# Seven products for twelve more pairs of a feed-forward, sixteen modulation steps moved to another one, and a new order in three short places

## The chip, the cores and the metric

The kernel is one program on one core of a Trainium2 chip. The metric is device time of that core in microseconds (us), the median of several executions. TensorE (PE in the profile, with PEld for its weight loads) does the matrix products, VectorE (DVE), ScalarE (ACT) and GpSimd (POOL) the elementwise work, and SyncE (SP) issues most of the transfers from the chip's memory into the on-chip buffer. Each engine takes its instructions in the order in which the program has them and waits at one whose inputs are not there.

## The reference, cut to what matters

Two layers work on 512 tokens, 256 latent ones (`x`) and 256 of context (`xc`), of width 1024. Each layer is a feed-forward, a mixing block and another feed-forward. All is fp32.

```
mod = (silu(c) @ ada_w[l] + ada_b[l])                 # nine vectors of 1024 per layer, for x and for xc
h   = rms(x) * (1 + mod[1]) + mod[0]
x   = x + 0.5 * mod[2] * ((silu(h @ wg) * (h @ wu)) @ wd)       # wg, wu: 1024 x 2816, wd: 2816 x 1024
h   = rms(x) * (1 + mod[4]) + mod[3]
x   = x + mod[5] * mixing(h)    # short and long convolution, gated chunk MLP, latent attention
x   = x + 0.5 * mod[8] * (second feed-forward, with mod[6], mod[7])
```

The chunk MLP of the mixing multiplies a normalised `v` (in the kernel `gv`) by a 128 x 128 matrix per group (in the kernel in `sg`). In the second layer the mixing and the last feed-forward need the latent tokens alone.

## The kernel before, in words

Tokens lie along the free dimension, features on the 128 partitions. The program runs its stages one after the other: first feed-forward (layer 0; `ffn(0,0)`), mixing, second feed-forward (`ffn(0,1)`), then for layer 1 the third feed-forward (`ffn(1,0)`), the last mixing and a fourth feed-forward over 256 tokens.

Every fp32 product is made of three products in a rounded fp32 format, high by high, low by high and high by low (`mm3`, lines 164 to 166). So each weight block is loaded into `raw` by a transfer that SP issues, cast to `whi` by ACT, and DVE makes `wlo` as `raw` minus `whi` (`split`, line 139). `raw`, `whi` and `wlo` have four buffers each.

A feed-forward cuts its 2816 inner columns into 22 blocks of 128. Block m is a pair of products, gate and up, each over eight blocks of 128 features: 2 x 8 x 3 = 48 matrix products of 512 columns. The pairs go in three chunks, 0 to 7, 8 to 14 and 15 to 21. After each chunk comes its down projection: eight output tiles d, each a sum over the chunk's blocks in a `dn` bank (two of them), after which DVE adds the tile to `x` (`residual`, line 583).

In the pairs that the table `SEVEN` lists, the pair's product with its 2 x 2 blocks of halves is made with seven block products in place of eight (the Strassen-Winograd form): 7 x 12 = 84 matrix products of 256 columns. It needs sums of the weights (`raw`, `ws`, `w3h`, `w3l`: DVE and POOL) and sums of `h`, as `th` and `tl`, which `forms` makes by four subtractions for each of four tiles. Before, `SEVEN` has 15 pairs of the third feed-forward alone.

Beside this, each feed-forward does a share of the modulation: 128 steps (`ada_sums`) in all. One step loads 512 KB of `ada_w` into `araw` (SP) and does two instructions on DVE, `asum <- araw, cc, asum`, one for each half of a vector's columns, or one where the vector is needed for latent tokens only. After every eighth step PE gathers the partitions with `pick` (line 239), and two transposes and a few small DVE operations make the modulation vector `modv`. `slot(n)`, called once per pair and once per down tile, does n steps. The four feed-forwards do 48, 40, 32 and 8 steps. The first two also make the filters of a mixing (`filters`, in buffers named `filt`), a little in each slot.

Across engines nothing else orders the work: within each engine the framework's scheduler places instructions by priorities and the dependencies, so the order on an engine can differ from the order of the code. The changed places are `ada_sums`, `full` and `forms` of the class `Modulated`, `ffn`, and the section of `mixing` with `short` (six projections for the short convolution, line 971), two projections for `gu` and the products with `sg` (line 992).

Of the kernel before, what the change touches and what calls it, by code (L numbers as in the profile page):

```python
# [26 lines left out]
SEVEN = {(1, 0): tuple(range(4, 7)) + tuple(range(8, 14)) + tuple(range(15, 21))}  # L27
# [57 lines left out]
def tile_trunk(ctx: ExitStack, tc: tile.TileContext, xT, cT, ada_f, ada_w, w_up, w_dn, w_in, w_v, w_uq, w_ukv, w_out,  # L85
# [123 lines left out]
    here, rows, sums = [], [], []  # L209
# [12 lines left out]
    def ada_sums(n, tile_of):  # L222

        for _ in range(n):
            l, m, k, raw = here.pop(0)
            S = halves_of(l, m)
            with queued(later):
# [7 lines left out]
            if k == KD - 1:  # L235
                p = bank("ad", 1)
                for s in range(S):
                    for q in range(4):
                        PE.matmul(p[32 * q:32 * q + 32, 0:256], lhsT=pick[:, s, :],
                                  rhs=sums[s][:, q * 256:(q + 1) * 256], start=(s == 0), stop=(s == S - 1))  # L240
                sums.clear()
                row = tp.tile([P, 256], F32, tag="arow", name="arow", bufs=2)
                A.copy(out=row, in_=p[:, :256])
                rows.append((l, m, row))
# [48 lines left out]
    class Modulated:  # L293
# [51 lines left out]
        def full(self, b, bc, k, anchors):  # L345
# [5 lines left out]
            for i in range(2):  # L351
                if self.keep is None:
                    t = tp.tile([P, 512], F32, tag="t0", name="nt")
                else:
                    t = self.kept[-1][:, i * 512:(i + 1) * 512]
                eng, src = (V, b) if k + i == 0 else (G, bc)
                eng.tensor_tensor(out=t[:, :T], in0=x[:, ks[i], :T], in1=src[:, :T], op=ALU.mult)  # L357
                ts.append(t)
            for i, t in enumerate(ts):
                for s, c in enumerate(halves(T)):  # L360
                    g, h = (modv[self.l][:, self.m + j, s, ks[i]:ks[i] + 1] for j in (1, 0))
                    if i == 0:
                        A.activation(t[:, c], t[:, c], AF.Identity, bias=h, scale=g)
                    else:
                        V.tensor_scalar(out=t[:, c], in0=t[:, c], scalar1=g, scalar2=h, op0=ALU.mult, op1=ALU.add)
# [4 lines left out]
        def forms(self, th, tl):  # L370
# [215 lines left out]
    def ffn(l, f, T, h, nxt, steps, side=None):  # L586

        m0 = 6 * f
        with ExitStack() as es:
            fx = es.enter_context(tc.tile_pool(name=f"side{l}{f}", bufs=1, reuse_waits="tile"))  # L590
            fpool = es.enter_context(tc.tile_pool(name=f"ffn{l}{f}", bufs=1, reuse_waits="tile"))
            fast = SEVEN.get((l, f), ())
            af = [fpool.tile([P, 8 * 516], F32R, name=n) for n in ("ah", "al")]
# [8 lines left out]
            def tile_b():  # L602
                return fx.tile([P, 1024], F32, tag="filt", name="filt", bufs=7)

            def tile_w():
                return fpool.tile([P, 1024], F32, tag="ws", name="ws", bufs=1)

            if fast:
                th = fpool.tile([P, 4, 1028], F32R, name="th")
                tl = fpool.tile([P, 4, 1028], F32R, name="tl")  # L610
# [8 lines left out]
            else:  # L619
                hh, hl = h.high, h.low  # L620
                n = 3 if T == 512 else 4
                if fast:
# [6 lines left out]
            def slot(n):  # L629
                ada_flush()  # L630
                for _ in range(min(n, left[0])):
# [5 lines left out]
                if n > 0 or calm == 2:  # L637
                    next(gen, None)

            def todo_light():  # L640
                return not here or halves_of(*here[0][:2]) == 1
# [9 lines left out]
            def copied(src):  # L651
                t = fpool.tile([P, 256], F32, tag="cp", name="cp", bufs=5)
# [720 lines left out]
```

## Time and profile before

| | |
|---|---|
| median of 3 executions | 1780.89 us (1779.01 to 1781.73) |
| the profiled execution: own time, span | 1781.89 us, 1780.1 us |
| busy share of the span | PE 97%, PEld 82%, DVE 71%, ACT 41%, POOL 14% |
| stages on the profile's clock | first feed-forward 0 to 423 us, mixing to 658, second feed-forward to 1046.6, third to 1415.4, last mixing to 1570, fourth feed-forward to the end |
| transferred | 254.65 MB, mean 143 GB/s |

Busy is the time in which an engine has an instruction under way; a busy PE is not one at its peak, since its clock is granted in levels. The span is the time from the profile's first instruction to its last; the own time is that of the same execution as the device reports it.

### The profile page before, as it was taken

What the parts mean: (1) busy time and instruction counts of PE and PEld (TensorE: products, weight loads), DVE (VectorE), ACT (ScalarE), POOL (GpSimd) and SP (SyncE); (2) the same over time, 40 slices, a digit from 0 to 9 for tenths busy, and PEclk for the clock granted to TensorE, in tenths of its full rate; (3) what the DMA queues carried; (4) which work ended last, traced back from release to release, by engine and by line L of the source; (5) the groups of instructions that cost most, each with busy time, mean ns of one, the idle gap of its engine ahead of it and who ended that gap; (6) DMA issues with size and microseconds to landing.
All of it is one profiled execution on the core that took longest, in us unless ns stands there. A gap on an engine that the chain in (4) does not pass through costs nothing.

```text
span 1780.1 us, 25745 instructions
## 1 busy us (share of the span) xinstructions
PE 1734.6 (97%) x9994; PEld 1453.6 (82%) x9994; DVE 1267.5 (71%) x1969; ACT 723.9 (41%) x1217; POOL 241.6 (14%) x196
## 2 busy tenths in 40 slices
PE   7999999999999999999999999999999989999998
PEld 5877777788876687777778887889799888789998
DVE  4787768647767669977753478778787697687555
ACT  5421222234534645222222346336245474564443
POOL 2101000003212022100000043012021231120001
PEclk9999999999999999999999999999999999999999
DMA  9464556423320044655542223553743432257563
GB/s 363 136 203 142 186 169 211 137 86 111 116 86 25 24 139 130 203 165 180 172 130 93 87 71 107 174 159 123 231 150 114 138 127 95 72 172 231 179 188 96
DMA packets 72319, 254.65 MB, mean 143 GB/s; under 512 B 8322, under 2 KB 9090, under 8 KB 71940
## 3 DMA queue, kind: packets, MB, share of 16 engines
q1 hardware_dynamic: 69408, 246.18, 42.7%
q10 hardware_dynamic: 2788, 6.81, 1.2%
q8 instruction: 79, 1.29, 0.3%
q14 instruction: 44, 0.36, 0.1%
HBM read 251.91 MB, written 1.05 MB: 142 GB/s over the span
## 4 chain that ended last, share of the span: by engine, by line
PE 86%; DVE 6%; issue 3%; ACT 2%; DMA 1%; POOL 1%; SPq 0%; ACTq 0%; DVEq 0%; POOLq 0%
PE mm L164 15%; PE mm L166 14%; PE mm L165 14%; PE dn L164 8%; PE dn L165 8%; PE dn L166 8%; PE mm L675 5%; PE dn L675 2%; DVE wlo L139 2%; PE mm L396 1%; PE mm L1099 1%; PE ad L1133 1%; PE ms L675 1%; DMA araw<-in_ada_w 1%; PE ms L1119 1%
## 5 line engine op out<-in xcount | busy, mean ns | idle before, releaser
L139 ACT CAST whi<-raw 128x1024 fp32r<-128x1024 f32 (+3 forms) x329 | 334.6, 1020 | 800.8 <-PE mm L165 279.8
L139 DVE TENSOR_TENSOR wlo<-raw,whi 128x1024 fp32r<-128x1024 f32 (+3 forms) x329 | 403.0, 1228 | 157.5 <-ACT whi L139 154.6
L164 PE MATMUL mm<-hh,whi 128*128 128x512 f32 (+2 forms) x1232 | 444.3, 361 | 8.5 <-DVE np L431 5.1
L166 PE MATMUL mm<-hh,wlo 128*128 128x512 f32 (+2 forms) x1232 | 441.8, 359 | 2.2 <-DVE wlo L139 2.1
L165 PE MATMUL mm<-hl,whi 128*128 128x512 f32 (+2 forms) x1232 | 440.1, 358 | 1.0 <-DVE hl L139 1.0
L164 PEld LDWEIGHTS mm<-hh,whi 128*128 128x128 f32 (+1 forms) x1232 | 232.1, 188 | 53.0 <-DVE np L431 5.7
L166 PEld LDWEIGHTS mm<-hh,wlo 128*128 128x128 f32 (+1 forms) x1232 | 232.4, 189 | 39.9 <-DVE wlo L139 4.0
L165 PEld LDWEIGHTS mm<-hl,whi 128*128 128x128 f32 (+1 forms) x1232 | 233.2, 189 | 37.3 <-DVE hl L139 1.8
L164 PE MATMUL dn<-ah,whi 128*128 128x512 f32 (+1 forms) x704 | 261.1, 371 | 0.0
L165 PE MATMUL dn<-al,whi 128*128 128x512 f32 (+1 forms) x704 | 258.5, 367 | 0.3
L166 PE MATMUL dn<-ah,wlo 128*128 128x512 f32 (+1 forms) x704 | 258.1, 367 | 0.0
L233 DVE SCALAR_TENSOR_TENSOR asum<-araw,cc,asum 128x1024 f32<-128x1024 f32 x196 | 249.0, 1304 | 7.2 <-DMA araw<-in_ada_w 7.0
L288 POOL TENSOR_TENSOR ssum<-ssum,sq 128x512 f32<-128x512 f32 (+1 forms) x42 | 53.1, 1265 | 886.3 <-ACT sq L287 886.1
L164 PEld LDWEIGHTS dn<-ah,whi 128*128 128x128 f32 x704 | 132.6, 189 | 29.0 <-issue 4.4
L165 PEld LDWEIGHTS dn<-al,whi 128*128 128x128 f32 x704 | 133.0, 189 | 24.5 <-DVE al L139 1.0
L166 PEld LDWEIGHTS dn<-ah,wlo 128*128 128x128 f32 x704 | 132.8, 189 | 23.6 <-issue 0.4
L583 DVE SCALAR_TENSOR_TENSOR x<-dn,modv,x 128x256 f32<-128x256 f32 x171 | 76.2, 479 | 95.4 <-PE dn L166 95.2
L647 DVE TENSOR_TENSOR a<-sg,mm 128x512 f32<-128x512 f32 (+1 forms) x67 | 40.5, 604 | 92.3 <-PE mm L166 92.3
L333 DVE SCALAR_TENSOR_TENSOR hl<-x,modv,hh 128x256 fp32r<-128x256 f32 x88 | 65.9, 789 | 2.3 <-ACT hh L327 2.3
L139 DVE TENSOR_TENSOR al<-a,ah 128x512 fp32r<-128x512 f32 (+1 forms) x88 | 57.4, 654 | 1.4 <-ACT ah L139 1.4
L139 ACT CAST ah<-a 128x512 fp32r<-128x512 f32 (+1 forms) x88 | 49.6, 566 | 20.5 <-DVE a L647 16.1
L357 POOL TENSOR_TENSOR nt<-x,bc 128x512 f32<-128x512 f32 (+1 forms) x35 | 46.9, 1350 | 81.2 <-ACT bc L420 37.7
(347 smaller groups left out, 2632.7 us busy)
## 6 DMA issues: line engine op xcount, KB each, us to landing
raw<-in_w_up SPq DMA_DIRECT2D x176, 512.0 KB, 3.6
araw<-in_ada_w SPq DMA_DIRECT2D x128, 512.0 KB, 4.0
raw<-in_w_dn SPq DMA_DIRECT2D x64, 448.0 KB, 3.3
raw<-in_w_dn SPq DMA_DIRECT2D x32, 512.0 KB, 4.4
raw<-in_w_in SPq DMA_DIRECT2D x26, 512.0 KB, 3.6
raw<-in_w_out SPq DMA_DIRECT2D x16, 512.0 KB, 3.3
filt<-in_ada_f SPq DMA_DIRECT2D x10, 512.0 KB, 8.3
raw<-in_w_uq SPq DMA_DIRECT2D x8, 384.0 KB, 3.0
```

Of the source, the lines that this page charges most:

```text
L139: return [A.copy(out=hi, in_=src).ins, V.tensor_tensor(out=lo, in0=src, in1=hi, op=ALU.subtract).ins]
L164: PE.matmul(o, lhsT=wh, rhs=ah, start=first, stop=False)
L165: PE.matmul(o, lhsT=wh, rhs=al, start=False, stop=False)
L166: PE.matmul(o, lhsT=wl, rhs=ah, start=False, stop=last)
L233: V.scalar_tensor_tensor(out=sums[s], in0=raw, scalar=cc[:, k, s:s + 1], in1=sums[s], op0=ALU.mult, op1=ALU.add)
L288: G.tensor_tensor(out=parts[0][:, :T], in0=parts[0][:, :T], in1=sq[:, :T], op=ALU.add)
L333: V.scalar_tensor_tensor(out=self.hl[:, k, o], in0=x[:, k, c], scalar=modv[self.l][:, self.m + 1, s, k:k + 1], in1=self.hh[:, k, o], op0=A ...
L357: eng.tensor_tensor(out=t[:, :T], in0=x[:, ks[i], :T], in1=src[:, :T], op=ALU.mult)
L396: PE.matmul(p[:, :258], lhsT=(wl if part == 1 else wh)[:, c], rhs=h, start=k == 0 and part == 0, stop=k == KD - 1 and part == 2)
L583: V.scalar_tensor_tensor(out=x[:, d, c], in0=psum[:, c], scalar=modv[l][:, m, s, d:d + 1], in1=x[:, d, c], op0=ALU.mult, op1=ALU.add)
L647: V.tensor_tensor(out=a[:, :T], in0=sg[:, :T], in1=got[m, 1][:, :T], op=ALU.mult)
L675: PE.matmul(p, lhsT=w[part == 2][:, o + k * P:o + (k + 1) * P], rhs=b(k)[part == 1], start=start and k == 0 and part == 0, stop=k == 3 and ...
```

## The change

Five things are changed:

- `SEVEN` also has 12 pairs of the second feed-forward, 8 to 13 and 15 to 20. There the buffers of the filters hold the space, so `th`, `tl`, `ws`, `w3h`, `w3l` and `cp` are placed in it after the first chunk (`late`). By then `h` is there only as `hh` and `hl`: `again` adds the two on POOL, tile by tile, and calls `forms` for each of the four tiles, during the first down projection. `araw` has two buffers there in place of three.
- The steps of modulation are 64, 24, 32 and 8, and where they stand is told by `in_up` and `in_down`.
- The gather with `pick` is no longer called behind the eighth step but at the next slot, at the next vector's first step, or at a chunk's end (`ada_ripe`). A slot makes its share of the filters first.
- In `full`, for the third feed-forward, the normalised tile goes to `t0` and from there, modulated, to the kept tile. In `forms` the first subtraction goes from POOL to DVE, and both first subtractions of all tiles are issued before the second ones.
- In the last mixing PE follows the order of the code from the short convolution to the products with `sg`.

```
-SEVEN = {(1, 0): tuple(range(4, 7)) + tuple(range(8, 14)) + tuple(range(15, 21))}
+SEVEN = {(0, 1): tuple(range(8, 14)) + tuple(range(15, 21)),
+         (1, 0): tuple(range(4, 7)) + tuple(range(8, 14)) + tuple(range(15, 21))}
...
             if k == KD - 1:
-                p = bank("ad", 1)
...
+                ripe.append((l, m))
+
+    def ada_ripe():
+        for l, m in ripe:
+            S = halves_of(l, m)
+            p = bank("ad", 1)
+            for s in range(S):
+                for q in range(4):
+                    PE.matmul(p[32 * q:32 * q + 32, 0:256], lhsT=pick[:, s, :],
+                              rhs=sums[s][:, q * 256:(q + 1) * 256], start=(s == 0), stop=(s == S - 1))
...
-                if self.keep is None:
-                    t = tp.tile([P, 512], F32, tag="t0", name="nt")
-                else:
-                    t = self.kept[-1][:, i * 512:(i + 1) * 512]
+                t = tp.tile([P, 512], F32, tag="t0", name="nt")
...
-            for k, w in enumerate(self.kept):
-                q = [w[:, i * 256:(i + 1) * 256] for i in range(4)]
-                G.tensor_tensor(out=q[0], in0=q[1], in1=q[0], op=ALU.subtract)
+            qs = [[w[:, i * 256:(i + 1) * 256] for i in range(4)] for w in self.kept]
+            for q in qs:
+                V.tensor_tensor(out=q[0], in0=q[1], in1=q[0], op=ALU.subtract)
                 G.tensor_tensor(out=q[1], in0=q[3], in1=q[1], op=ALU.subtract)
+            for k, q in enumerate(qs):
                 V.tensor_tensor(out=q[3], in0=q[3], in1=q[0], op=ALU.subtract)
                 V.tensor_tensor(out=q[2], in0=q[2], in1=q[3], op=ALU.subtract)
-                split(th[:, k, 0:1024], tl[:, k, 0:1024], w)
+                split(th[:, k0 + k, 0:1024], tl[:, k0 + k, 0:1024], self.kept[k])
...
             def slot(n):
+                if n > 0 or calm == 2:
+                    next(gen, None)
                 ada_flush()
+                ada_ripe()
...
-            def todo_light():
-                return not here or halves_of(*here[0][:2]) == 1
+            def in_up(m):
+
+                if m in fast or m < calm or f == 0 and l == 1 and m < 7:
+                    return 0
+                return 3 if l == 1 and f == 0 and m == 21 or l == 0 and f == 0 and m % 2 == 1 else 2
+
+            def in_down(ch, d):
+
+                last = ch == len(CHUNKS) - 1
+                if not fast:
+                    return 0 if last else 1
+                if l == 0:
+                    return 1 if ch == 0 and d >= 4 or ch == 1 and d < 4 else 0
+                if last:
+                    return 1 if d < 4 else 0
+                if ch == 1:
+                    return 2 if d < 5 else 1 if d == 5 else 0
+                return 2 if here and halves_of(*here[0][:2]) == 1 else 1
...
+            def again():
+
+                for k in range(4):
+                    w = tile_w()
+                    for i in range(2):
+                        G.tensor_tensor(out=w[:, i * 512:(i + 1) * 512], in0=hh[:, k + 4 * i], in1=hl[:, k + 4 * i],
+                                        op=ALU.add)
+                    yield
+                    h.kept = [w]
+                    h.forms(th, tl, k)
+                    yield
...
-                    slot(2 if m >= (7 if fast else calm) else 0)
+                    slot(in_up(m))
...
+                if late and ch == 0:
+                    for _ in gen:
+                        pass
+                    filt.close()
+                    fp[0] = es.enter_context(tc.tile_pool(name=f"fast{l}{f}", bufs=1, reuse_waits="tile"))
+                    th, tl = sums_of_h()
+                    more = again()
...
-                    slot(0 if end else 2 if fast and todo_light() else 1)
+                    for _ in range(2):
+                        next(more, None)
+                    slot(in_down(ch, d))
...
+            order = ExitStack()
+            if last:
+                order.enter_context(tc.manual_schedule(engines={PE_}))
...
-    h = ffn(0, 0, 512, None, (0, 3, 512), 48, lambda tile_of: filters(0, tile_of))
+    h = ffn(0, 0, 512, None, (0, 3, 512), 64, lambda tile_of: filters(0, tile_of))
...
-    h = ffn(0, 1, 512, h, (1, 0, 512), 40, lambda tile_of: filters(1, tile_of))
+    h = ffn(0, 1, 512, h, (1, 0, 512), 24, lambda tile_of: filters(1, tile_of))
```

On DVE, at tiles d = 2 and 3 of the second feed-forward's first down projection, the order before is the one below. `x <- dn` is the residual of a tile d (two halves), `wlo` the low half of a coming weight, `asum` a modulation step.

```order
L583 SCALAR_TENSOR_TENSOR x<-dn,modv_82,x 128x256 x2
L139 TENSOR_TENSOR wlo<-raw,whi 128x1024
L583 SCALAR_TENSOR_TENSOR x<-dn,modv_82,x 128x256 x2
L231 TENSOR_SCALAR asum<-araw,cc 128x1024 x2
L233 SCALAR_TENSOR_TENSOR asum<-araw,cc,asum 128x1024 x4
```

With the change, at tiles d = 0 and 1 of the same down projection (the `ws` rows are the three DVE subtractions of `forms`, `tl` the low half of the sums of `h`):

```order
L593 SCALAR_TENSOR_TENSOR x<-dn,modv_82,x 128x256
L140 TENSOR_TENSOR wlo<-raw,whi 128x1024
L140 TENSOR_TENSOR tl<-ws,th 128x1024
L236 SCALAR_TENSOR_TENSOR asum<-araw,cc,asum 128x1024
L384 TENSOR_TENSOR ws<-ws 128x256
L593 SCALAR_TENSOR_TENSOR x<-dn,modv_82,x 128x256
L387 TENSOR_TENSOR ws<-ws 128x256
L593 SCALAR_TENSOR_TENSOR x<-dn,modv_82,x 128x256
L388 TENSOR_TENSOR ws<-ws 128x256
L140 TENSOR_TENSOR wlo<-raw,whi 128x1024
L236 SCALAR_TENSOR_TENSOR asum<-araw,cc,asum 128x1024
L140 TENSOR_TENSOR tl<-ws,th 128x1024
```

Per tile d the four DVE instructions of one round of `again` have come in between the residuals and the `wlo`; some residuals and each `wlo` now stand behind a `ws` subtraction.

On PE, in the third feed-forward's second down projection, the gather of a modulation vector (`ad <- asum, pick`) stood before inside tile d = 5 (`dn_10671`), behind three of its products (whose rows repeat the pattern of three):

```order
L165 MATMUL dn_10628<-al_8323,whi_10624 128x512
L166 MATMUL dn_10628<-ah_8322,wlo_10625 128x512
L164 MATMUL dn_10671<-ah_8322,whi_10667 128x512
L165 MATMUL dn_10671<-al_8323,whi_10667 128x512
L166 MATMUL dn_10671<-ah_8322,wlo_10668 128x512
L239 MATMUL ad_10656<-asum_10543,pick_86 32x256 x4
L164 MATMUL dn_10671<-ah_8322,whi_10667 128x512
```

Now it stands between the last product of tile d = 5 (`dn_11486`) and the first of d = 6 (`dn_11527`):

```order
L166 MATMUL dn_11486<-al_9137,whi_11482 128x512
L167 MATMUL dn_11486<-ah_9136,wlo_11483 128x512
L247 MATMUL ad_11508<-asum_11361,pick_86 32x256 x4
L165 MATMUL dn_11527<-ah_9136,whi_11523 128x512
L166 MATMUL dn_11527<-al_9137,whi_11523 128x512
```

So the gather has moved 18 products back, from the start of the tile to its end.

On PE, in the last mixing, the first products with `sg` stood before between the projections of the short convolution, in front of those of the block `mm_12636`, and the last ones behind the projections:

```order
L166 MATMUL mm_12598<-hh_11659,wlo_12595 128x256
L992 MATMUL dn_12810<-sg_11982,gv_11983 64x128 x3
L164 MATMUL mm_12636<-hh_11659,whi_12632 128x256
...
L166 MATMUL mm_12782<-hh_11659,wlo_12779 128x256
L992 MATMUL dn_12810<-sg_11982,gv_11983 64x128
L992 MATMUL dn_12818<-sg_11982,gv_11983 64x128 x4
L164 MATMUL mm_12842<-kh_11972,whi_12837 128x512
```

With the change all eight stand behind the last projection (`mm_13606`):

```order
L166 MATMUL mm_13606<-hl_12461,whi_13602 128x256
L167 MATMUL mm_13606<-hh_12460,wlo_13603 128x256
L1052 MATMUL dn_13634<-sg_12804,gv_12805 64x128 x4
L1052 MATMUL dn_13642<-sg_12804,gv_12805 64x128 x4
L165 MATMUL mm_13667<-kh_12794,whi_13662 128x512
```

Three products have moved from the middle of the projections to their end.

## Rows read from the trace of the kernel before

**Rows 1.** The page, busy time: engine, us, share of the span, instructions.
```profile
PE 1734.6 (97%) x9994; PEld 1453.6 (82%) x9994; DVE 1267.5 (71%) x1969; ACT 723.9 (41%) x1217; POOL 241.6 (14%) x196
```
**Rows 2.** Windows: stretch, us, engines' busy (instructions), clock, transfer share, GB/s.
```profile
71.10:131.80 60.70, 60.70 (x269) 46.43 (x267) 55.08 (x67) 23.16 (x36) 2.80 (x2) 1.00 0.60 192
759.50:808.10 48.60, 48.60 (x217) 37.60 (x216) 36.20 (x46) 10.21 (x13) 0.00 (x0) 1.00 0.54 167
808.10:889.00 80.90, 80.90 (x374) 64.07 (x373) 54.59 (x58) 21.95 (x30) 0.00 (x0) 1.00 0.52 170
889.00:929.40 40.40, 40.40 (x189) 32.13 (x187) 25.26 (x37) 8.74 (x11) 0.00 (x0) 1.00 0.42 136
929.40:1007.60 78.20, 78.20 (x338) 63.15 (x337) 25.34 (x28) 21.32 (x28) 0.00 (x0) 1.00 0.29 91
1046.60:1141.00 94.40, 89.48 (x589) 80.88 (x588) 75.32 (x105) 50.53 (x86) 27.72 (x21) 1.00 0.32 101
1187.30:1257.70 70.40, 70.40 (x554) 68.29 (x553) 52.95 (x67) 37.87 (x63) 13.43 (x9) 1.00 0.38 116
1257.70:1305.00 47.30, 43.76 (x191) 33.86 (x190) 38.81 (x46) 9.91 (x13) 3.39 (x3) 0.93 0.75 244
```
**Rows 3.** Waits of PE: what waited, for what: us in total, times, longest.
```profile
PE mm L164 <- DVE np L431: 5.1, 3, 1.9
PE ad L239 <- DVE asum L233: 3.5, 2, 3.2
PE mm L166 <- DVE wlo L139: 2.4, 3, 1.4
PE dn L992 <- DVE z L971: 2.1, 1, 2.1
...
PE mm L164 <- ACT hh L139: 1.3, 1, 1.3
PE mm L675 <- ACT cp L653: 1.1, 1, 1.1
PE dn L992 <- POOL gv L956: 0.6, 1, 0.6
```
**Rows 4.** Timeline of PE: start, us, instruction, [idle before, releaser].
```profile
1287.46 1.08 PE L239 MATMUL ad<-asum,pick 128*32 128x256 f32 x8 [3.24 <-DVE asum L233]
```
**Rows 5.** Windows behind this wait and behind that for `z` in the last mixing.
```profile
1287.50:1297.00 9.50, 9.50 (x37) 6.98 (x38) 7.73 (x11) 2.04 (x3) 1.28 (x1) 0.71 0.73 238
1468.10:1475.00 6.90, 6.90 (x50) 6.86 (x50) 2.41 (x6) 1.51 (x2) 0.00 (x0) 0.82 0.20 71
```
**Rows 6.** Timeline of DVE in the third feed-forward's second down projection.
```profile
1286.12 1.28 DVE L233 SCALAR_TENSOR_TENSOR asum<-araw,cc,asum 128x1024 f32<-128x1024 f32 x1 [0.88 <-DMA araw<-in_ada_w]
```
**Rows 7.** The page, costliest groups: busy us, mean ns, idle before.
```profile
L139 ACT CAST whi<-raw 128x1024 fp32r<-128x1024 f32 (+3 forms) x329 | 334.6, 1020 | 800.8 <-PE mm L165 279.8
L139 DVE TENSOR_TENSOR wlo<-raw,whi 128x1024 fp32r<-128x1024 f32 (+3 forms) x329 | 403.0, 1228 | 157.5 <-ACT whi L139 154.6
...
L233 DVE SCALAR_TENSOR_TENSOR asum<-araw,cc,asum 128x1024 f32<-128x1024 f32 x196 | 249.0, 1304 | 7.2 <-DMA araw<-in_ada_w 7.0
...
L583 DVE SCALAR_TENSOR_TENSOR x<-dn,modv,x 128x256 f32<-128x256 f32 x171 | 76.2, 479 | 95.4 <-PE dn L166 95.2
```
**Rows 8.** Groups of the third feed-forward's start (1046.6 to 1141 us).
```profile
L357 POOL TENSOR_TENSOR asum<-x,bc 128x512 f32<-128x512 f32 x4 | 5.6, 1424 | 0.0
...
L375 POOL TENSOR_TENSOR asum<-asum 128x256 f32<-128x256 f32 x2 | 2.3, 1150 | 3.5 <-DVE hl L139 3.5
```
**Rows 9.** Groups of DVE in the last mixing (1450 to 1476 us).
```profile
L969 DVE SCALAR_TENSOR_TENSOR z<-mm,ppt,z 128x127 f32<-128x127 f32 x8 | 2.7, 343 | 0.1
```
**Rows 10.** Groups of DVE at the third feed-forward's start.
```profile
L703 DVE TENSOR_TENSOR cp<-ms,cp 128x256 f32<-128x256 f32 x3 | 1.2, 415 | 0.3 <-PE ms L675 0.3
```
**Rows 11.** Timeline of DVE, second feed-forward's start, then third's.
```profile
668.45 2.60 DVE L139 TENSOR_TENSOR hl<-nt,hh 128x512 fp32r<-128x512 f32 x2
...
1058.02 3.47 DVE L139 TENSOR_TENSOR hl<-ws,hh 128x512 fp32r<-128x512 f32 x2
```

More of the change, by code (lines that the diff above doesn't have):

```diff
@@ L208, in tile_trunk @@
     todo = [(l, m, k) for l in range(DEPTH) for m in (0, 1, 2, 3, 4, 7, 5, 6, 8) for k in range(KD)][2 * KD:]
-    here, rows, sums = [], [], []
+    here, rows, sums, ripe = [], [], [], []
     def halves_of(l, m):
@@ L235, in ada_sums @@
             if k == KD - 1:
-                p = bank("ad", 1)
[L237 to L244, printed above, removed]
+                ripe.append((l, m))
[7 more added lines that the diff above has]
+                              rhs=sums[s][:, q * 256:(q + 1) * 256], start=(s == 0), stop=(s == S - 1))
+            sums.clear()
+            row = tp.tile([P, 256], F32, tag="arow", name="arow", bufs=2)
+            A.copy(out=row, in_=p[:, :256])
+            rows.append((l, m, row))
+        ripe.clear()
     def ada_flush():
@@ L361, in full @@
                     g, h = (modv[self.l][:, self.m + j, s, ks[i]:ks[i] + 1] for j in (1, 0))
+                    o = t[:, c] if self.keep is None else self.kept[-1][:, i * 512 + s * 256:i * 512 + (s + 1) * 256]
                     if i == 0:
[L363 removed]
+                        A.activation(o, t[:, c], AF.Identity, bias=h, scale=g)
                     else:
[L365 removed]
+                        V.tensor_scalar(out=o, in0=t[:, c], scalar1=g, scalar2=h, op0=ALU.mult, op1=ALU.add)
+            if self.keep is not None:
+                ts = [self.kept[-1][:, i * 512:(i + 1) * 512] for i in range(2)]
             for i, t in enumerate(ts):
@@ L592, in ffn @@
             fast = SEVEN.get((l, f), ())
+            late = len(fast) > 0 and side is not None
+            filt = es.enter_context(ExitStack())
+            fp = [filt.enter_context(tc.tile_pool(name=f"filt{l}{f}", bufs=1, reuse_waits="tile")) if late else fpool]
             af = [fpool.tile([P, 8 * 516], F32R, name=n) for n in ("ah", "al")]
@@ L602, in tile_b, with sums_of_h @@
             def tile_b():
-                return fx.tile([P, 1024], F32, tag="filt", name="filt", bufs=7)
+                return (fp[0] if late else fx).tile([P, 1024], F32, tag="filt", name="filt", bufs=7)
             def tile_w():
[L606 to L610, printed above, removed]
+                return fp[0].tile([P, 1024], F32, tag="ws", name="ws", bufs=1)
+            def sums_of_h():
+                return [fp[0].tile([P, 4, 1028], F32R, name=n) for n in ("th", "tl")]
+            if fast and not late:
+                th, tl = sums_of_h()
             tiles = [(m, j) for m in range(MF) for j in range(2)]
@@ L621, in ffn @@
                 n = 3 if T == 512 else 4
-                if fast:
+                if fast and not late:
                     h.keep = [tile_w, tile_s, tile_s, tile_a]
@@ L651, in copied @@
             def copied(src):
-                t = fpool.tile([P, 256], F32, tag="cp", name="cp", bufs=5)
+                t = fp[0].tile([P, 256], F32, tag="cp", name="cp", bufs=5)
                 A.copy(out=t, in_=src)
@@ L691, in seven @@
                 ws = parts(ws)
-                w3 = [fpool.tile([P, 512], F32R, tag=n, name=n) for n in ("w3h", "w3l")]
+                w3 = [fp[0].tile([P, 512], F32R, tag=n, name=n) for n in ("w3h", "w3l")]
                 V.tensor_tensor(out=a11, in0=a11, in1=a21, op=ALU.subtract)
@@ L701, in seven @@
                 sg = tp.tile([P, 512], F32, tag="t0", name="sg")
-                ut = fpool.tile([P, 256], F32, tag="cp", name="cp", bufs=5)
+                ut = fp[0].tile([P, 256], F32, tag="cp", name="cp", bufs=5)
                 V.tensor_tensor(out=ut, in0=b2, in1=p1, op=ALU.add)
@@ L775, in ffn @@
                         squares(d, T, parts)
+            ada_ripe()
+            ada_flush()
             assert left[0] == 0
```

12 lines of the change are left out of this document (8 added, 4 removed).

## The prediction

> **What bounds the kernel now.** I read the page's busy shares first: PE is busy 97% of the span, 45.5 us are left [rows 1]. So there are two ways to gain: fewer PE cycles, or one of the few places where PE waits. Then the table of windows, one row for each chunk's pairs and each down projection [rows 2]. The reader is to see that in six of its eight rows PE's busy time equals the stretch to the last digit at a clock of 1.00: nothing but PE's own work sets the time there, whatever DVE does. The two others are the start of the third feed-forward (94.40 us with 89.48 busy) and its second down projection (47.30 with 43.76, mean clock 0.93). Next, PE's waits by what they wait for [rows 3], the longest of interest in the timeline [rows 4], and the windows behind it and behind the wait for `z` [rows 5]: after 3.24 us without work the granted clock is 0.71 over 9.5 us, after 2.1 us it is 0.82 over 6.9 us, a mixture of the upper level (2.4 GHz) and the half. So a wait costs its length and a piece behind it: (1 - 0.71) x 9.5 = 2.8 us and (1 - 0.82) x 6.9 = 1.2 us.
>
> **The change part by part.** The profiled execution took 1781.9 us, 1.0 over the median. The sum is made against the first, and 1.0 is taken off at the end.
>
> *Seven products in the second feed-forward.* Its third chunk is seven plain pairs with no modulation beside them: 78.20 us, or 11.17 a pair. The third feed-forward's second chunk has six pairs of seven products and a plain one: 70.40 us, so (70.40 - 11.17) / 6 = 9.87 [rows 2]. Each of the 12 pairs saves 1.30 us: **-15.5 us**. These rows carry the term because PE is never idle in them although the weight sums run beside it: DVE is busy 52.95 of 70.40 us, POOL 13.43. The second feed-forward will have what the third has, and one modulation step less or more. Bounds: 0 if the weight sums fail to keep up (below), and -15.5, since PE cannot do better than rows without an idle moment.
>
> *Rebuilding the sums of h.* In the first down projection there are now four rounds: two POOL additions (1.42 us each), three subtractions on DVE (0.415 each, a row of that size) with one on POOL (1.15) beside them, a cast of 1024 columns (1.02) and a DVE subtraction of 1024 columns (1.23) [rows 7, 8, 10]. End to end a round is 2.84 + 1.25 + 1.02 + 1.23 = 6.3 us. A tile d takes PE 48.60 / 8 = 6.07 us. DVE was busy 36.20 of 48.60 us; it loses four of the eight steps that the slots there did (4 x 2 x 1.30 = 10.4) and gains 4 x (1.25 + 1.23) = 9.9: 35.7 us, 12.9 us free. What DVE queues behind a subtraction that waits for POOL are two residuals and a `wlo`. A residual frees one of two `dn` banks, so it may be late by one tile, 6.07 us, and each `wlo` has a buffer in hand. I cost it at **0**; PE's own products are the cover. If the cover is gone, a round shows for what it lasts beyond the tile, bounded by 6.3 us and the clock piece of 2.8.
>
> A row bears on this cover: two subtractions of 512 columns take DVE 2.60 us with POOL idle and 3.47 us with POOL at work, a third more [rows 11]. Over POOL's 8 x 1.42 + 4 x 1.15 = 16.0 us that is some 5.3 us of DVE time, 41.0 of 48.60 us, still hidden. The Trainium skill (SBUF — State Buffer, "Who interferes with whom") is harsher: a DVE instruction with two inputs in the on-chip buffer shares a read interface with GpSimd, and of the pair that it shares one holds all and the other "fully blocks". In this pair of rows the trace does not go that far; what full turns would do here is the second rival.
>
> *Steps moved to the first feed-forward.* Sixteen steps, each two DVE instructions of 1.304 us [rows 7] and a load of 512 KB on SP's queue. `in_up` gives the odd pairs 3 instead of 2: three more in the first chunk, three in the second, ten in the third. First chunk: 55.08 us of DVE in 60.70 us [rows 2], plus 3 x 2.61 = 7.8: 62.9, so DVE falls 2.2 us behind, against a lead of several `wlo`. The second is like the second feed-forward's with steps, 54.59 of 80.90: 62.4. The third is like the row without steps, 25.34 of 78.20, plus 18 steps, 47.0: 72.3. Both fit. Transfers are at a share of 0.60 in the first chunk; 3 x 0.52 MB on 192 GB/s x 60.7 us = 11.7 MB makes it 0.68. I take **+1.0**, half of the overload, bounds 0 and +3 (2.2 and a first piece of clock). The two gathers and their transposes move from the second feed-forward to the first and cancel on PE: (80.90 - 78.20) / 2 = 1.35 us each [rows 2].
>
> *Third feed-forward, second down projection.* The like stretch of the second one takes 40.40 us with 189 products, this one 47.30 with 191 [rows 2]: 6.9 us are to be had at most. The gather waited 3.24 us for the last `asum` at d = 5, and that `asum` was itself late by its load (0.88 us, transfers at a share of 0.75) [rows 2, 4, 6]. Now 18 products stand between, 0.23 us each (78.20 / 338 in the stretch of plain pairs): 4.2 us, so the gather finds its sums with 0.9 us in hand. Idle time 47.30 - 43.76 = 3.54 and the piece of clock 2.8: **-6.3**. Bounds -6.9, and 0 if the loads come a microsecond later.
>
> *Third feed-forward, start.* PE idles 94.40 - 89.48 = 4.9 us there [rows 2]: the waits for `hh` (1.3) and `cp` (1.1) and the longest for `np` and `wlo` [rows 3]. POOL, which does seven normalisations of 1.42 us and eight subtractions of some 1.15 [rows 8], hands four subtractions to DVE: 4 x 0.415 = 1.7 us more there, against 4 x 1.15 = 4.6 us in which DVE runs a third slower [rows 11], and the chain of the sums no longer alternates between the two engines. The `np` wait ends with work that no edit touches. Of the 2.4 us for `hh` and `cp` I take most: **-2.0**; bounds -4.9 and +1.7 (the added DVE time in full).
>
> *Last mixing.* The two waits for `gv` and `z` (0.6 + 2.1) [rows 3] come from products with `sg` that PE took between the projections although their inputs were not ready; in the order of the code they stand behind eight projections. With 1.2 us of clock [rows 5]: **-3.9**. The wait added is that PE may not pass over a projection whose weight or bank is not ready, and behind it queue all later ones. A projection's 24 products of 256 columns are a quarter of a pair, 2.8 us; DVE does on one a `wlo` (1.23) and, for six of the eight, six `z` instructions of at most 0.34 [rows 7, 9]: 3.3 us, so it falls up to 0.5 behind at each of six, 3.0 in all, against a lead of some `wlo`. Bounds -4.4 and +3.
>
> Sum: -15.5 + 0 + 1.0 - 6.3 - 2.0 - 3.9 = -26.7. 1781.9 - 26.7 = 1755.2, on the median's basis **1754.2 us**. With every term at its good end (-15.5, 0, 0, -6.9, -4.9, -4.4) it would be -31.7, 1749.2.
>
> **The rivals.**
>
> *The waits only move (1766.4 us).* PE waits for inputs that are late whatever its order: the gather's `asum` is late by its load, and `gv` and `z` by DVE. If all three places keep their loss, -15.5 + 1.0 = -14.5 is left. For it: the transfers at 0.75 and the `asum` released by one. Against it: the gather has 18 products more, the products with `sg` all projections.
>
> *DVE and POOL take full turns (1760 us).* If DVE stands still for all of POOL's 16.0 us in the rebuilding stretch, it is at 35.7 + 16.0 = 51.7 of 48.60 us, 3.1 late; PE waits that and loses 2.8 of clock: -26.7 + 5.9 = -20.8. Against it: the third more of the rows, where full turns would have been more. It decides once POOL's 16 us cost DVE more than 12.9.
>
> *The seven products gain nothing (1769.7 us).* The weight sums come later than PE wants them in the second feed-forward, which also carries modulation: -26.7 + 15.5 = -11.2. Against it: the third feed-forward does this and a step at some of these pairs without an idle moment.
>
> *Slower: each round of the rebuilding shows (1790 us).* One mechanism, in the second feed-forward's first down projection: POOL's additions wait for the tile's single buffer `ws`, which the round before holds to its last `tl`; DVE stands at the subtraction behind them with the residual in its queue; PE finds no free `dn` bank and no `wlo`. Four rounds of 6.3 and the clock piece of 2.8 after each are 36.4 us: 1755.2 + 36.4 = 1791.6, 1790.6 on the median. It turns slower once more than 26.7 / 4 - 2.8 = 3.9 us of each round stands open, that is, once a residual is over 6.07 + 3.9 = 10 us late. Against it: a round is 6.3 us and the bank of a tile gives 6.07.
>
> **How the numbers follow.** Forecast 0.71, its own range 1748 to 1759 (the good ends, and +5 for the loads or the first feed-forward). Waits that move 0.13 (some of them, mostly: 1758 to 1767), full turns 0.08, no gain of the seven products 0.03, slower 0.05. The range from 1746 to 1770 us takes in all of these but the last, and at the low end 3 us for prices that the rows give only by likeness. What a measurement of this kernel can tell from no change is 0.2%, 3.6 us. Above 1777.3 and within 3.6 of the median only a part of the slower case falls, 0.01; slower 0.04; faster 0.95.
>
> **What would show it.** Second feed-forward: stretches of some 70.4 us for the second and third chunk's pairs (the second with one or two steps' gather more), PE without idle time. First down projection 48 to 49 us, no row of PE waiting for `ws`, `tl` or a `dn` bank. Third feed-forward: second down projection near 41 us at a clock of 1.00, the gather without a wait in front. Last mixing: no wait at the products with `sg`. First feed-forward: unchanged within 2 us; a new row of PE waiting for `wlo` there would be its overload. I am wrong if PE's idle time outside these places has grown, if the 12 pairs take over 10.2 us each, or if the waits of the third feed-forward and the last mixing are there under another name.

## The result, and the profile after

The changed kernel takes 1761.47 us (median of 4 runs, 1760.32 to 1762.57) against 1781.31 us of the kernel before (4 runs, 1779.01 to 1783.02). The ratio is 0.9889, 95% interval 0.9872 to 0.9906: faster by 19.8 us, where 26.7 were forecast (1754.2 us). The time lies in the wide range of 1746 to 1770 us, but not in that of the forecast itself, 1748 to 1759. The profiled execution took 1760.32 us, span 1758.5 us: 21.6 us less than the one of before, while the medians differ by 19.8.

The windows of the changed kernel, cut at the same stage borders as [rows 2]: stretch, us, busy of PE, PEld, DVE, ACT and POOL (instructions), clock, transfer share, GB/s.

```profile
762.40:816.40 54.00, 50.17 (x216) 38.45 (x214) 47.36 (x63) 15.04 (x17) 18.82 (x14) 0.97 0.41 124
816.40:887.20 70.80, 70.80 (x558) 68.72 (x555) 52.90 (x70) 37.03 (x63) 13.43 (x9) 1.00 0.38 114
...
926.20:996.70 70.50, 70.50 (x554) 68.39 (x553) 52.72 (x68) 37.92 (x62) 12.99 (x8) 1.00 0.39 114
...
1038.10:1131.50 93.40, 89.69 (x582) 80.23 (x582) 75.51 (x108) 50.06 (x86) 23.62 (x17) 1.00 0.34 102
1248.10:1289.50 41.40, 41.23 (x189) 32.07 (x188) 33.10 (x43) 9.52 (x12) 3.88 (x3) 1.00 0.74 239
```

The second and fourth stretch of the second feed-forward in [rows 2], 80.90 and 78.20 us, are 70.80 and 70.50, with PE busy throughout. The second down projection of the third feed-forward is 41.40 in place of 47.30, its start 93.40 in place of 94.40 (93.8 when cut at the first product). One stretch has become longer: the second feed-forward's first down projection, 48.60 before, is 54.00 with PE busy for 50.17 of it at a clock of 0.97 (before, cut like this one at the first products of the two stages, it is 48.2). It is the one that carries the rebuilding.

PE's waits of the changed kernel (what waited, for what: us in total, times, longest):

```profile
PE mm L165 <- DVE np L441: 3.1, 2, 1.7
...
PE dn L165 <- DVE x L593: 2.2, 2, 2.0
...
PE mm L707 <- ACT cp L685: 1.9, 2, 1.4
PE ms L890 <- DVE kre L896: 1.8, 1, 1.8
...
PE mm L166 <- DVE hl L140: 1.7, 3, 0.8
...
PE mm L165 <- DVE z L1028: 0.8, 1, 0.8
```

Against [rows 3], the rows of the gather (`ad <- asum`) and of the products with `sg` are gone. New are the waits for a residual (`x`, 2.0 of the 2.2 us) and for `kre`, both in the first down projection of the second feed-forward, and a wait of 0.8 us for `z` in the last mixing, at another product than before.

In that down projection, DVE's timeline (start, us, instruction, idle before and its releaser) shows the rounds. `L384`, `L387` and `L388` are the three subtractions of a round on DVE:

```profile
771.52 0.42 DVE L384 TENSOR_TENSOR ws<-ws 128x256 f32<-128x256 f32 x1
771.86 1.28 DVE L236 SCALAR_TENSOR_TENSOR asum<-araw,cc,asum 128x1024 f32<-128x1024 f32 x1
773.76 0.43 DVE L387 TENSOR_TENSOR ws<-ws 128x256 f32<-128x256 f32 x1 [0.63 <-POOL ws L385]
...
779.97 1.49 DVE L384 TENSOR_TENSOR ws<-ws 128x256 f32<-128x256 f32 x1 [1.19 <-POOL ws L763]
781.39 0.47 DVE L593 SCALAR_TENSOR_TENSOR x<-dn,modv,x 128x256 f32<-128x256 f32 x1
782.38 0.42 DVE L387 TENSOR_TENSOR ws<-ws 128x256 f32<-128x256 f32 x1 [0.52 <-POOL ws L385]
...
788.42 1.49 DVE L384 TENSOR_TENSOR ws<-ws 128x256 f32<-128x256 f32 x1 [0.63 <-POOL ws L763]
...
797.41 1.49 DVE L384 TENSOR_TENSOR ws<-ws 128x256 f32<-128x256 f32 x1 [0.59 <-POOL ws L763]
```

The rounds begin at 771.5, 780.0, 788.4 and 797.4 us: 8.5 to 9.0 us apart, where a tile takes PE 6.07. DVE waits seven times for POOL, once in the first round and twice in each of the others, and three times a subtraction that takes 0.42 us alone takes 1.49. POOL's timeline of the same time shows why:

```profile
777.66 3.52 POOL L763 TENSOR_TENSOR ws<-hh,hl 128x512 f32<-128x512 f32 x2 [3.93 <-DVE tl L140]
781.61 0.74 POOL L385 TENSOR_TENSOR ws<-ws 128x256 f32<-128x256 f32 x1 [0.43 <-DVE ws L384]
787.08 2.54 POOL L763 TENSOR_TENSOR ws<-hh,hl 128x512 f32<-128x512 f32 x2 [4.73 <-DVE tl L140]
```

In the second round POOL's two additions wait for the round before (`tl`, the buffer's last reader) and end at 781.18 us; DVE's subtraction, free to go from 779.97 since it needs the first addition alone, ends at 781.46. It got through only when POOL was done, and so in the two rounds behind it, each time 0.28 to 0.29 us after POOL's second addition. DVE's waits in this stretch, then in the same stretch of the kernel before:

```profile
DVE ws L384 <- POOL ws L763: 2.4, 3, 1.2
DVE ws L387 <- POOL ws L385: 2.4, 4, 0.6
```

```profile
DVE x L583 <- PE dn L166: 11.4, 4, 3.6
```

Before, DVE waited 11.4 us for PE, which is its lead. After, it waits for POOL and no longer for PE: the lead is used up. PE waits 1.8 us for `kre` (for the filters' last products, which now stand at the start of this projection in one piece) and 2.0 for `x`, and the 10 us from 792 to 802, around the second wait, have a granted clock of 0.83. So 54.00 - 50.17 = 3.8 us are idle, and PE is busy 50.17 us in place of 48.2, of which (1 - 0.83) x 10 = 1.7 are the clock.

### The profile page after: what moved, and what is told of

Its sections match the earlier page's. It is cut to its first block, busy times and chain, and to the rows that moved or that the text cites. A ratio compares the mean times of both kernels' runs of the same rounds, so it can differ in the third digit from the quotient of the medians.

```text
span 1758.5 us, 26921 instructions
## 1 busy us (share of the span) xinstructions
PE 1714.2 (97%) x10426; PEld 1458.4 (83%) x10426; DVE 1336.7 (76%) x2073; ACT 761.2 (43%) x1293; POOL 292.9 (17%) x228
## 5 line engine op out<-in xcount | busy, mean ns | idle before, releaser
L165 PE MATMUL mm<-hh,whi 128*128 128x512 f32 (+1 forms) x1040 | 367.7, 354 | 7.1 <-DVE np L441 3.1
L167 PE MATMUL mm<-hh,wlo 128*128 128x512 f32 (+1 forms) x1040 | 365.5, 352 | 1.5 <-DVE wlo L140 1.4
L166 PE MATMUL mm<-hl,whi 128*128 128x512 f32 (+1 forms) x1040 | 364.4, 350 | 1.7 <-DVE hl L140 1.7
L165 PEld LDWEIGHTS mm<-hh,whi 128*128 128x128 f32 x1040 | 195.2, 188 | 41.3 <-issue 4.3
L167 PEld LDWEIGHTS mm<-hh,wlo 128*128 128x128 f32 x1040 | 195.3, 188 | 31.1 <-DVE wlo L140 3.5
L166 PEld LDWEIGHTS mm<-hl,whi 128*128 128x128 f32 x1040 | 196.1, 189 | 29.6 <-DVE hl L140 3.1
L721 POOL TENSOR_TENSOR ws<-ws,raw 128x512 f32<-128x512 f32 x27 | 47.7, 1768 | 291.6 <-DVE ws L720 179.7
L363 POOL TENSOR_TENSOR nt<-x,bc 128x512 f32<-128x512 f32 (+1 forms) x42 | 58.1, 1395 | 91.2 <-ACT bc L430 44.1
L679 DVE TENSOR_TENSOR a<-sg,mm 128x512 f32<-128x512 f32 (+1 forms) x55 | 32.2, 587 | 45.1 <-PE mm L167 45.1
L707 PE MATMUL mm<-th,whi 128*128 128x256 f32 x216 | 61.1, 283 | 1.9 <-ACT cp L685 1.9
```

Of the source, the lines that this page charges most:

```text
L165: PE.matmul(o, lhsT=wh, rhs=ah, start=first, stop=False)
L166: PE.matmul(o, lhsT=wh, rhs=al, start=False, stop=False)
L167: PE.matmul(o, lhsT=wl, rhs=ah, start=False, stop=last)
L679: V.tensor_tensor(out=a[:, :T], in0=sg[:, :T], in1=got[m, 1][:, :T], op=ALU.mult)
L707: PE.matmul(p, lhsT=w[part == 2][:, o + k * P:o + (k + 1) * P], rhs=b(k)[part == 1], start=start and k == 0 and part == 0, stop=k == 3 and ...
L721: G.tensor_tensor(out=s2, in0=s1, in1=a11, op=ALU.subtract)
```

## Experiments

Theory A: the 5.8 us of the first down projection come from the hand-over between DVE and POOL. Theory B: DVE has too much work there, whoever does what. The first three runs were made to tell them apart, and the first of them does; most of the others undo one part each.

**The rounds on DVE alone.**

```
-                        G.tensor_tensor(out=w[:, i * 512:(i + 1) * 512], in0=hh[:, k + 4 * i], in1=hl[:, k + 4 * i],
+                        V.tensor_tensor(out=w[:, i * 512:(i + 1) * 512], in0=hh[:, k + 4 * i], in1=hl[:, k + 4 * i],
...
-                G.tensor_tensor(out=q[1], in0=q[3], in1=q[1], op=ALU.subtract)
+                (V if k0 or len(qs) == 1 else G).tensor_tensor(out=q[1], in0=q[3], in1=q[1], op=ALU.subtract)
```

> Edit: POOL's share of the rebuilding (eight additions and four subtractions) is done on DVE. Theory A (hand-over): DVE gets 4 x (2 x 0.69 + 0.42) = 7.2 us more work, but its waits for POOL (6 x 0.6 + 1.2) and three lengthened subtractions (3 x 1.07), together 8.0 us, go: the wait for x is about 2 us or less, 52 to 54 us in the down projection, time 1760 to 1761.5 us. Theory B (work): 7 us more of work come out as wait: about 60 us there, time 1768 us.

Measured: 1757.78 us (1756.79 to 1759.67), ratio to before 0.987 (0.9853 to 0.9886). The stretch is 48.30 us:

```profile
763.70:812.00 48.30, 48.30 (x217) 37.29 (x215) 46.09 (x71) 15.17 (x17) 2.60 (x2) 1.00 0.36 112
```

DVE's timeline there shows a round without idle time, its additions 0.64 us each where POOL's took 1.27 to 2.28 in the changed kernel:

```profile
778.10 1.28 DVE L763 TENSOR_TENSOR ws<-hh,hl 128x512 f32<-128x512 f32 x2
779.30 0.42 DVE L384 TENSOR_TENSOR ws<-ws 128x256 f32<-128x256 f32 x1
...
780.03 0.41 DVE L385 TENSOR_TENSOR ws<-ws 128x256 f32<-128x256 f32 x1
```

DVE takes over twelve instructions and is busy for 46.09 of 48.30 us, and PE has no idle moment. Theory B is out. A held too, beyond its own figure: it had left 2 us of wait, and none is left. What the run does not separate is DVE's waits for POOL from the subtractions that POOL held: it removes both. The stretch is 5.7 us shorter than in the changed kernel and the time only 3.7; in its profiled execution the start of the fourth feed-forward takes 3.2 us more, at a lower clock (last section).

**Stage buffers for the additions.**

```
+                ws = [add(k) for k in range(3)]        # three buffers of a pool of their own
                 for k in range(4):
                     yield
-                    h.kept = [w]
+                    h.kept = [ws[k]]
                     h.forms(th, tl, k)
+                    if k == 0:
+                        ws.append(add(3))
```

> Edit: the sums of h are staged in three buffers of their own, so that POOL's additions for the next rounds no longer wait for the round before. Theory A (hand-over): the first down projection of the second feed-forward took 54.0 us in place of 48.3 because in each round DVE waits for POOL and is held by POOL's additions, which makes a round 9.0 us against 6.07 for a tile; then the 2.0 us wait for x and its 1.9 us of clock go, 1.8 us (PE's wait at the filters' last products) stay: 50.2 us there, time 1757.7 us. Theory B (DVE simply has too much work there, 47.4 of 54.0 us): the work is the same, so the wait for x stays: 53 to 54 us, time 1761 us.

Measured: 1765.46 us (1765.15 to 1766.46), ratio to before 0.9916 (0.9901 to 0.993): 4.0 us slower than the changed kernel. The stretch is 48.60 us, but it is no test of A against B, since work left it together with the waits: the subtractions of three of the four rounds ran at the start of the second feed-forward, and DVE is busy for 40.93 us in the stretch in place of 47.36. The loss came out at that start, so that the down projection begins at 771.2 us in place of 762.4. Windows of the staged kernel, then POOL's timeline at the earlier one, and one of DVE's three subtractions there:

```profile
673.00:704.00 31.00, 25.34 (x130) 20.96 (x129) 29.98 (x38) 16.76 (x34) 19.66 (x14) 0.89 0.23 69
771.20:819.80 48.60, 48.35 (x217) 37.27 (x215) 40.93 (x52) 15.05 (x17) 10.32 (x7) 1.00 0.39 126
```

```profile
673.78 1.74 POOL L763 TENSOR_TENSOR ws<-hh,hl 128x512 f32<-128x512 f32 x1
675.48 1.34 POOL L363 TENSOR_TENSOR nt<-x,bc 128x512 f32<-128x512 f32 x1
676.78 1.34 POOL L763 TENSOR_TENSOR ws<-hh,hl 128x512 f32<-128x512 f32 x1
```

```profile
676.89 1.51 DVE L384 TENSOR_TENSOR ws<-ws 128x256 f32<-128x256 f32 x1
```

Freed from the buffer, the additions went in as soon as `hh` and `hl` were there, between the normalisations (`L363`) for which the first products wait: PE is busy 25.34 of 31.00 us at a clock of 0.89 (30.80 at 1.00 in the changed kernel). The wait for the single buffer had kept POOL out of a place where it is needed. So the miss in time is a new wait and says nothing against A.

**The filters' last piece earlier.**

```
                     slot(in_up(m))
+                    if late and m == 2:
+                        next(gen, None)
```

> Edit: one more piece of the filters is made in the slot of pair 2 of the second feed-forward, so that none is left for the chunk's end. Theory A: PE's 1.8 us wait at the filters' last products, inside the first down projection, goes and nothing takes its place: 52.2 us there, time 1759.7 us. Rival: DVE is the late engine in this stretch, so PE saves 1.8 us at its start and waits 1.8 us more for x: 54 us, time 1761.5 us.

Measured: 1761.34 us (1759.14 to 1763.75), ratio 0.9892 (0.9877 to 0.9907): no change that can be measured. The wait for `kre` is gone and the wait for `x` has become longer (3.2 us of the row below lie in the stretch, 2.0 in the changed kernel):

```profile
PE dn L165 <- DVE x L593: 3.5, 3, 2.0
```

The stretch is 50.4 us, but 1.2 us of the 3.6 that it lost are the filters' products that moved in front of it, and some 1.9 are the piece at lower clock, which its profiled execution does not have. Idle time is 3.3 us in place of 3.8. The rival had it: DVE's delay is what PE meets, at one instruction or another.

**No seven products in the second feed-forward.**

```
-SEVEN = {(0, 1): tuple(range(8, 14)) + tuple(range(15, 21)),
-         (1, 0): ...
+SEVEN = {(1, 0): ...
```

> Edit: the table of seven products without the twelve pairs of the second feed-forward; all else as in the changed kernel. By the sum of rows: 12 x 1.30 = 15.5 us come back, and the first down projection falls by the 5.7 us that the rebuilding and the flushed filters cost: net +9.8 us, time 1771.3 us. If the seven products gain nothing (rival): time 1755.8 us or below.

Measured: 1772.24 us (1770.45 to 1772.67), ratio 0.9951 (0.9936 to 0.9966), 10.8 us over the changed kernel where 9.8 were expected.

```profile
763.00:811.40 48.40, 48.40 (x218) 37.55 (x217) 39.95 (x52) 10.02 (x13) 0.00 (x0) 1.00 0.56 184
811.40:890.90 79.50, 79.50 (x355) 63.60 (x354) 31.44 (x36) 21.58 (x28) 0.00 (x0) 1.00 0.32 99
929.80:1008.00 78.20, 78.20 (x338) 63.12 (x338) 25.35 (x28) 21.31 (x28) 0.00 (x0) 1.00 0.28 90
```

Without the twelve pairs the down projection is 48.40 us again: the whole 5.6 us belongs to them and to what the code does for them alone (the rounds, the filters finished early, the steps of modulation in other places). The pairs give 79.50 + 78.20 - 70.80 - 70.50 = 16.4 us, of which some is a gather that stands elsewhere.

**The last mixing in the scheduler's order.**

```
-            if last:
+            if False:
                 order.enter_context(tc.manual_schedule(engines={PE_}))
```

> Edit: the changed kernel without the order of the code for PE in the last mixing. Theory (order): the products with sg stand between the projections again and wait 2.7 us, with 1.2 us of clock behind: from the start of the last mixing to the first product of the attention's scores 73.6 us becomes 77.5 us, time 1761.5 + 3.9 = 1765.4 us. Rival (gv and z are late whatever the order): the stretch stays at 73.6 us, time 1761.5 us.

Measured: 1766.87 us (1765.61 to 1768.18), ratio 0.9915 (0.99 to 0.9929). The wait is back at the products with `sg`, and so is the stretch up to the attention's scores; the second row is the changed kernel's stretch:

```profile
PE dn L1052 <- DVE z L1028: 2.1, 1, 2.1
```

```profile
1401.20:1478.70 77.50, 71.30 (x536) 68.01 (x536) 62.09 (x156) 45.12 (x80) 23.04 (x20) 0.96 0.41 132
```

```profile
1400.80:1474.40 73.60, 68.16 (x536) 65.05 (x537) 60.53 (x156) 45.15 (x80) 24.04 (x20) 1.00 0.44 140
```

3.9 us, as both the forecast and the expectation have it. The order of the code is what took the wait away. The time is 5.4 us longer, 1.5 more than expected; in the profiled execution the start of the fourth feed-forward is longer too, 54.9 in place of 51.8 us at a clock of 0.94 (last section).

**The gather at once.**

```
                 ripe.append((l, m))
+                ada_ripe()
```

> Edit: the gather with pick is called right behind the eighth step again; the new table of steps stays. Theory (the gather's place is what counts): in the third feed-forward's second down projection PE waits some 3 us for asum and loses up to 2.8 us of clock: 41.4 us there become 44 to 47 us, time 1764 to 1767.5 us. Rival (the new table of steps did it): 41 to 42 us, time 1761.5 us.

Measured: 1771.68 us (1765.71 to 1771.97), ratio 0.993 (0.9913 to 0.9948), 4 us above the expected range. In the third feed-forward's second down projection the wait is back, with the new table of steps unchanged (window, then PE's timeline):

```profile
1251.80:1298.20 46.40, 42.66 (x189) 33.21 (x189) 33.78 (x43) 9.81 (x12) 5.16 (x4) 0.96 0.65 213
```

```profile
1281.88 0.64 PE L248 MATMUL ad<-asum,pick 128*32 128x256 f32 x8 [3.26 <-DVE asum L236]
```

46.40 against 41.40 us: the gather's place is what counts. The rebuilding stretch takes 57.3 in place of 54.0 us as well. There PE waits 3.2 us for `kre` and 2.3 for `x`, and not for `asum`; how the gather's place leads to that is not shown.

**The old sums in the third feed-forward.** `full` writes the kept tiles directly and `forms` does its first subtraction on POOL, tile by tile, as in the diff's removed lines; the second feed-forward's rounds stay as changed.

> Edit: in the third feed-forward full and forms as before (normalised tiles written to the kept tiles, first subtraction on POOL, tile by tile). By the two traces: its first chunk of pairs takes 93.8 us in place of 93.4, time +0.4 us. By the forecast: +2.0 us. Rival: the edit gains nothing, 93.4 us.

Measured: 1763.92 us (1762.86 to 1765.89), ratio 0.9899 (0.9885 to 0.9914), which overlaps with that of the changed kernel. The stretch:

```profile
1039.10:1133.00 93.90, 88.90 (x582) 80.31 (x582) 74.83 (x104) 50.49 (x86) 27.75 (x21) 1.00 0.33 99
```

93.90 against 93.40 us, with 5.0 us idle against 3.7. The edit is worth 0.5 us there, not 2.0. Whether it is worth more in the time is open: the medians differ by 2.5 us, the intervals overlap, and of the 2.6 us between the two profiled spans the start of the fourth feed-forward, at a clock of 0.97 over 60 us, accounts for (1 - 0.97) x 60 = 1.8.

**Fourteen pairs.** The rounds on DVE, and pairs 14 and 21 also with seven products.

```
-SEVEN = {(0, 1): tuple(range(8, 14)) + tuple(range(15, 21)),
+SEVEN = {(0, 1): tuple(range(8, 22)),
...
+                for _ in prev:
+                    pass
                 ada_ripe()
...
-                    return 1 if ch == 0 and d >= 4 or ch == 1 and d < 4 else 0
+                    return 1 if ch == 0 and d >= 4 or ch == 1 else 0
```

> Edit: the rounds of rebuilding on DVE, and seven products also for pairs 14 and 21 of the second feed-forward, whose steps go to its second down projection. By the price of a pair: 2 x 1.30 = 2.6 us under the kernel with the rounds on DVE alone (1757.8 us): 1755.2 us. Rival: without a plain pair behind it, the last seven-product pair of a chunk finishes alone, PE waits for its last weight and then for the gate's result: the two chunks take as long as before or up to 4 us more each, time 1758 to 1766 us.

Measured: 1755.5 us (1754.15 to 1757.37), ratio 0.9852 (0.9837 to 0.9866), the lowest median here, 2.3 us under the one with the rounds on DVE, where 2.6 were expected; the two intervals overlap.

```profile
811.30:882.40 71.10, 71.10 (x601) 70.64 (x597) 56.80 (x76) 40.15 (x69) 19.34 (x12) 1.00 0.38 117
882.40:921.20 38.80, 38.80 (x181) 30.59 (x179) 36.65 (x44) 9.92 (x11) 2.59 (x2) 1.00 0.49 153
921.20:992.30 71.10, 71.10 (x601) 70.65 (x598) 58.93 (x78) 40.26 (x71) 19.35 (x12) 1.00 0.38 118
```

PE has no idle moment; the scheduler puts products of the down projection in front of the last pair's end.

## Why the prediction was right in direction and short in size

Term by term, by the two profiled executions (forecast, then measured; stretches are cut at their first products, which moves a border by some 0.1 us and, at the third feed-forward's start, by 0.6 against [rows 2]):

| term | forecast | measured | from |
|---|---|---|---|
| twelve pairs | -15.5 | -14.9 | 80.8 + 78.1 to 70.8 + 70.5 us, less the two gathers (2.7) that left these stretches |
| rebuilding | 0 | +5.8 | 48.2 to 54.0 us |
| steps moved to the first feed-forward | +1.0 | 0 | it ends 2.7 us later, the price of its two gathers on PE |
| third feed-forward, second down projection | -6.3 | -5.9 | 47.3 to 41.4 us |
| third feed-forward, start | -2.0 | -0.4 | 93.8 to 93.4 us |
| last mixing | -3.9 | -3.9 | 77.5 to 73.6 us |
| fourth feed-forward's start | 0 | -2.8 | 54.6 to 51.8 us, clock alone (below) |

Measured, these make -22.1; the spans differ by 21.6. The forecast's 12 x 1.30 is 15.6 and not 15.5, a slip without weight. Of the gain, 2.8 us are luck: no term foresaw the clock at the fourth feed-forward's start, and without it 18.8 us would be left of 21.6, where 26.7 were forecast.

*The step that was mis-sized is the rebuilding of the sums of h, costed at 0.* Its working put the round at 6.3 us end to end and DVE at 35.7 us, with 12.9 free. The trace after has DVE busy for 47.36 us, and PE waits for a residual, that is for a `dn` bank, where the prediction expected no such row. Three things were missed. First, DVE's own backlog: until 771.6 us, over nine us into the projection, it is still at `asum` and the last filters, and six more `asum` stand between the rounds, so that it goes into them without the lead that the row of 11.4 us shows for the kernel before. Second, the hand-over: POOL, DVE, POOL, DVE and ACT in one round, with a single buffer that keeps POOL from working ahead. DVE waits 4.8 us in all for POOL and is held 3 x 1.07 = 3.2 us by it. The kernel with the rounds on DVE alone shows that it is the hand-over that decides, since all of the loss goes though DVE gets more instructions. Third, [rows 11] were misread. POOL is not idle in the row of 2.60 us: it runs 1.29 us inside it. The same pair with POOL idle takes 1.28 us, 17 us later in the same trace:

```profile
669.20 1.29 POOL L357 TENSOR_TENSOR nt<-x,bc 128x512 f32<-128x512 f32 x1 [1.15 <-DVE hl L139]
```

```profile
685.86 1.28 DVE L139 TENSOR_TENSOR hl<-nt,hh 128x512 fp32r<-128x512 f32 x2
```

So the price of POOL beside it was not a third: 1.28 became 2.60 us, which is 1.28 + 1.29 to 0.03 us, and 3.47 in the other row. The trace before already showed the two engines taking turns, and the forecast had counted that as evidence against it.

The rival of full turns said 1760 us, and the time is 1761.5. Its mechanism is borne out at three instructions: the subtraction of 0.42 us takes 1.49, and each ends 0.28 to 0.29 us after POOL's addition. The Trainium skill (SBUF — State Buffer, "Who interferes with whom") has this for a DVE instruction with two inputs in the on-chip buffer next to a GpSimd instruction that reads it; here the trace agrees, with these three subtractions and with the pairs of 1.28 and 2.60 us above. But the rival's sum, all 16 us of POOL on DVE's account, isn't what happened: DVE was never at its limit of time, it stood idle 6.6 of 54.0 us. The slower rival named the right place and the right wait, a residual behind the subtraction; the residual was late by 2 us once, not by 10 us at each round.

*Steps moved.* That the first feed-forward takes them without a wait was right, and the 1.0 us for an overload was not needed: DVE's busy time in that feed-forward has risen from 287.7 to 323.1 us, and PE's idle time is 2.7 us as it was.

*The third feed-forward's second down projection* was right in mechanism and size: the gather runs at 1278.46 us with no wait in front, at a clock of 1.00.

*The third feed-forward's start* was right in direction alone: the waits for `np` and `wlo` are gone there and that for `hh` is shorter, but `cp` (1.9), `hl` and `sg` took their place; 4.9 us of idle time became 3.7, of which 0.4 us came out in the stretch (PE's busy time is longer in it, for as many products). That is the rival of waits that move, true for this place and, with the 0.8 us for `z`, for a part of the last mixing.

*The last mixing* was right to the tenth in the sum, and the experiment that undoes it gives the same 3.9. How the sum splits was not right. The stretch from 41 us behind the last mixing's start to the attention's scores, before and after:

```profile
1457.00:1493.50 36.50, 33.81 (x247) 31.44 (x247) 27.93 (x79) 16.03 (x24) 9.39 (x10) 0.95 0.45 153
```

```profile
1441.80:1474.40 32.60, 31.84 (x248) 30.06 (x247) 26.43 (x79) 15.97 (x24) 10.35 (x10) 1.00 0.54 170
```

PE's idle time fell from 2.7 to 0.8 us, since a wait of 0.8 for `z` is left at another product, and its busy time by 2.0, most of it clock ((1 - 0.95) x 36.5 = 1.8): 1.9 and 2.0 in place of 2.7 and 1.2. That the two errors cancel is luck.

## What to carry to other kernels

Time a piece of side work by the engines that it crosses, not by the sum of its instructions: four rounds through POOL, DVE and ACT with one buffer between them ran at 8.5 to 9.0 us each where the instructions add up to 6.3, and moving everything to the busier engine was faster. Before work is freed from a wait, look at what else its engine then does earlier: the staged additions landed among those that PE waits for. Take the price of an instruction alone from a row in which the other engine's timeline is seen to be empty. A product on sums that come from another engine can be moved behind products that are ready: here 18 of them covered the wait.

## What had not been expected of the hardware

The granted clock of a stretch differs between traces with the same waits. The start of the fourth feed-forward, 407 products and waits of 1.7, 1.5 and 0.8 us in each (the changed kernel has one of 0.2 more), in the kernel before, the changed one and the one with the rounds on DVE:

```profile
1571.70:1626.30 54.60, 52.21 (x407) 50.80 (x408) 43.49 (x72) 28.48 (x55) 5.58 (x7) 0.94 0.62 199
```

```profile
1552.60:1604.40 51.80, 49.33 (x407) 47.94 (x407) 43.18 (x70) 28.57 (x56) 5.57 (x7) 1.00 0.65 209
```

```profile
1549.20:1604.20 55.00, 52.52 (x407) 50.89 (x407) 43.31 (x70) 28.60 (x56) 5.58 (x7) 0.94 0.62 200
```

2.8 to 3.2 us hang on it that no edit here explains: the staged kernel and the one with the filters earlier have 1.00 there as well, all other traces less. Each trace is one execution of another kernel, so whether the execution or the kernel decides is not shown. The four runs of the changed kernel have a mean clock of 0.996 to 0.997 and those of the kernel with the rounds on DVE 0.993 to 0.994, which speaks for the kernel. With the gather at once three runs take 1771.42 to 1771.97 us at 0.991 to 0.993 and one takes 1765.71 at 0.996, which shows that executions of one kernel differ too. The price of a wait is its length and sometimes, not always, a piece at the half level behind it; the sum here counted such a piece as certain in two places, where it did come back.
